# Gathering expert tokens as one native float32 product, a fourth buffer of low halves, and a lookahead that skips unsplit weights

## Chip, cores and metric

One core of one Trainium2 chip. The metric is device microseconds (us) of one execution, the median of the runs. Engines are named as in the profile: PE (TensorE; PEld is its weight load), DVE (VectorE), ACT (ScalarE), POOL, SP (issues DMAs).

## The reference, cut to what matters

Two decoder layers on 256 tokens of width 1024, all float32. Layer 0 is a pooling and sliding-window attention mixer and a dense SwiGLU; layer 1 is a dilated attention and convolution mixer and a mixture of experts. Every sub-layer ends in `x <- LayerNorm(ALPHA * x + f(x))`. The change lies in the mixture of experts:

```
logits = xt @ w_router                          # 8 experts
top_logit, top_e = lax.top_k(logits, 2)
gates = softmax(top_logit)
for each expert e, on the rows xb of the tokens that chose it:
    y = (silu(xb @ w_gate[e]) * (xb @ w_up[e])) @ w_down[e]     # 1024 -> 3584 -> 1024
    out[token] += gate * y
```

All 24 matrices of 8 experts are read from HBM once: 336 pieces of 1 MB.

## The kernel before, in words

**Split products.** A float32 operand is cut into a high half `hi` (rounded to fp32r by a copy on ACT) and a low half `lo = src - hi` (a subtraction on DVE); `split` (lines 126 to 128) does both. A product is then hi·hi + lo·hi + hi·lo, three fp32r matmuls (`mm3`, lines 316 to 319). A *native* product takes float32 operands as they are.

**Weights.** `Weights` streams 128x2048 pieces. `load` issues a DMA on SP into a free `raw` tile; `hi` (L251 to 264; the copy is L259) writes the high half to a ring `wh` of AHEAD + 1 = 4 tiles on ACT; `lo` (the subtraction is L276) writes the low half to a ring `wl` of AHEAD = 3 tiles on DVE, and only then gives the raw tile back to the next DMA. `take` hands a piece to the matmuls, `drop` ends it: it counts `used` up and calls `pump`, which issues one `hi` and one `lo`. This order of issue is the order of work on ACT and on DVE, since the part is scheduled by hand (`tc.manual_schedule`, L1049): each engine runs its instructions in the order of the program. The limits, for a piece k of the experts:

```
            if k in self.native or k not in self.raw or k - self.used > ahead or k >= self.limit:
                return False
...
                if k - self.used < AHEAD - 1 if k >= MOE_BASE else self.step(self.at_lo) != self.at_hi:
                    self.lo()
```

The first is in `hi`, which `pump` calls with `ahead` = 2; the second in `pump`. So `hi` runs up to two pieces beyond `used`, `lo` up to one. Pieces 0 to 3 of the experts are split in two halves each (so `pump` runs twice for them). Twenty of the 336 pieces are *native* (not split; L1225 uses them from the raw tile): the down matrices of every second step of the heavy experts, and one piece of most steps of the last light one.

**Experts.** After routing, experts are sorted by their number of tokens. Expert 0 comes first; those with at most 64 tokens are *light* (five here: 1 to 5), others (0, 6, 7) *heavy*. A step (`Experts.step`) is one 512-wide slice of one expert: two gate pieces, two up pieces, then the two down pieces of the step before. Heavy and light steps alternate in an order fixed by `mixed`. A heavy step ends its up product with a multiplication on DVE (L1438, `h`), and PE transposes `h` after the two down pieces (L1243). In the very first step there is no step before, so the transposes follow at once; behind them DVE runs some 25 small instructions that sort the experts (L1317 to L1355).

**Gather.** A unit (`Unit`, L1162) holds the gathered tokens of one expert, split into high and low halves. A one-hot matrix `oh` of token against slot is the moving operand; the stationary one is a 128x128 block of the tokens. Because the tokens are split once, into `xkh` and `xkl` (two 128x2048 fp32r tiles; L1090, L1092, L1116, L1302), the gather runs twice: a product for the high halves and one for the low halves, each 16 matmuls, all at L1180. A heavy unit does this in four parts with a PSUM bank each (`half`, evacuated by three ACT copies and one DVE copy at L1186), a light one in two (`thin`, two ACT copies at L1191). `Experts.part` runs one part after the gate product and one after the up product of a step. Banks come from a ring of four, shared with the gate and up products, the fold of the light steps (L1237, a native float32 product) and the combine (L1280 to L1282).

**Order around routing.** Lines 1070 to 1118 and 1285 to 1310 lay out by hand the norm of both token halves, the router's transposes and logits, the token splits, and single `W.hi()` and `W.lo()` calls between them. Then `x` is scaled by ALPHA in place (L1323) and collects the experts' results. At the end seven matmuls on `xkh` (L1509) keep PE running before the last merge.

Of the kernel before, what the change touches and what calls it, by code (L numbers as in the profile page):

```python
# [26 lines left out]
PIECE = 2048  # L27
# [61 lines left out]
def trunk(ctx, tc, stream, x_tok, x_t, pos, ln_w, ln_b, pool_bd, pool_sc, sinks, conv_w, router, cf, cb, windows,  # L89
# [64 lines left out]
    class Weights:  # L154
        def __init__(self):
            self.order = []
            self.native, self.base = set(), [0]
            self.raw, self.split, self.loaded = {}, {}, 0
            self.free = [raw1.tile([128, PIECE], F32, name=f"raw{i}") for i in range(RAW1)]
            self.kept = {}  # L160
            self.limit = LIMIT
            self.taken = self.used = 0
            self.at_hi = self.at_lo = (0, 0)

        def follow(self, seq, native=()):
            order = list(range(MOE_BASE + 4))
            for s in range(1, len(seq)):
                order += [(*seq[s], j) for j in range(4)] + [(*seq[s - 1], j) for j in (4, 5)]
            order += [(*seq[-1], j) for j in (4, 5)]
            assert order[:self.loaded] == self.order[:self.loaded]  # L170
            self.order = order
            self.native = {k for k, o in enumerate(order) if o in native}

        def skip(self):
# [76 lines left out]
        def hi(self, ahead=AHEAD):  # L251
            self.skip()
            k, q = self.at_hi
            if k in self.native or k not in self.raw or k - self.used > ahead or k >= self.limit:
                return False
# [27 lines left out]
        def pump(self, n=1, full=False):  # L283
            for _ in range(n):
                self.hi(AHEAD if full else AHEAD - 1)
                k = self.at_lo[0]
                if k - self.used < AHEAD - 1 if k >= MOE_BASE else self.step(self.at_lo) != self.at_hi:
                    self.lo()
# [599 lines left out]
    with tc.tile_pool(name="od1", bufs=1) as e1, tc.tile_pool(name="od2", bufs=2) as e2:  # L888
# [153 lines left out]
    raw3 = ctx.enter_context(tc.tile_pool(name="raw3", bufs=1))  # L1042
    xk, yb = [raw2.tile([128, PIECE], F32R, name=f"xk{i}") for i in range(2)], \
        raw2.tile([128, PIECE], F32R, name="yb")
    raws = [raw3.tile([128, PIECE], F32, name=f"raw{RAW1 + i}") for i in range(RAW2 + RAW3 - 3)]
# [3 lines left out]
    ctx.enter_context(tc.manual_schedule())  # L1049
    xkh, xkl = [t.rearrange("p (i d) -> p i d", i=2) for t in xk]  # L1050
    lgp = bank()
    lg0 = lgp[:, :2 * NE].rearrange("p (i e) -> p i e", e=NE)

    def route(norm, c):
# [10 lines left out]
        return logits  # L1065

    def split_tokens(i):
        split(xkh[:, i], xkl[:, i], x[:, i])

# [19 lines left out]
    lga = route(na, 4)  # L1089
    nc.scalar.copy(xkh[:, 0], x[:, 0])  # L1090
    lgb()
    nc.vector.tensor_sub(xkl[:, 0], x[:, 0], xkh[:, 0].bitcast(F32))  # L1092
    lgb = route(na, 6)
# [21 lines left out]
    keep(KEEP[2])  # L1115
    nc.scalar.copy(xkh[:, 1], x[:, 1])  # L1116
    W.hi()
# [44 lines left out]
    class Unit:  # L1162
# [13 lines left out]

        def gather(self, a, c, b, m):
            for k in range(c, c + 512 // m):
                for i in range(2):
                    nc.tensor.matmul(b[:, (k - c) * m:(k - c + 1) * m],  # L1180
                                     (xkh, xkl)[a][:, i, k * 128:(k + 1) * 128],
                                     self.oh[:, i], start=i == 0, stop=i == 1)

        def half(self, c, a, b, copy):
            self.gather(a, c, b, 128)
            copy(self.xg[a][:, c:c + 4], b.rearrange("p (k s) -> p k s", s=128))  # L1186

        def thin(self, a):
            b = bank()
            self.gather(a, 0, b, LIGHT)  # L1190
            nc.scalar.copy(self.xg[0][:, :, a * LIGHT:(a + 1) * LIGHT], b.rearrange("p (k s) -> p k s", s=LIGHT))  # L1191

        def parts(self):
            yield self.start()
            for j in range(2 if self.light else 4):
                if self.light:
                    self.thin(j)
                else:
                    self.half(4 * (j % 2), j // 2, bank(), nc.vector.tensor_copy if j == 3 else nc.scalar.copy)
                yield  # L1200

# [86 lines left out]
    m2 = ctx.enter_context(tc.tile_pool(name="mo2", bufs=1, side="right"))  # L1288
    rings.add("oh", [m2.tile([128, 2, 128], F32R, name="oh")])
    rings.add("ohb", [m2.tile([128, 2, 128], F32R, name="ohb")])  # L1290
# [7 lines left out]
    rings.add("bank", [bank() for _ in range(4)])  # L1298
    places = [big_tile(t) for t in ("mh", "ml")]
    unit = Unit(places[0], 0, False, slot)  # L1300
    unit.start()
    nc.vector.tensor_sub(xkl[:, 1], x[:, 1], xkh[:, 1].bitcast(F32))  # L1302
    W.lo()
    for c in (0, 4):
        unit.half(c, 0, acc(), nc.scalar.copy)
    for c in (0, 4):
        unit.half(c, 1, bank(), nc.vector.tensor_copy if c == 0 else nc.scalar.copy)
    for _ in range(4):
# [7 lines left out]
    def gates():  # L1316
# [5 lines left out]
        nc.vector.tensor_add(gate, gate, hots[1])  # L1322
        nc.scalar.activation(x, x, AF.Copy, scale=ALPHA)  # L1323

# [178 lines left out]
    def tail(x8):  # L1503
# [4 lines left out]
        for _ in range(7):  # L1508
            nc.tensor.matmul(spare, xkh[:, 0, :128], xkh[:, 0, :512], start=True, stop=True)  # L1509
        e, n, ht = x8.prev  # L1510
# [207 lines left out]
```

## Time and profile before

| | us |
|---|---|
| runs | 1370.35, 1371.65, 1372.81 (median 1371.65) |
| profiled execution, its own time | 1369.15 |
| its span, first to last instruction | 1367.4 |
| mean granted TensorE clock | 0.993 of 2.4 GHz |

The mixer of layer 0, its SwiGLU and the mixer of layer 1 take the first 440 us; routing and the first gather lie at 440 to 470 us; the experts at 470 to 1345 us; the last norm and output after that. In rows of the timeline the columns are start, duration, engine, line, operation, out<-in and shape; what stands in brackets is the idle time of the engine before it and what ended it. In rows by group, the numbers after the bar are total busy time in us and the mean of one in ns, then idle time before.

### The profile page before, as it was taken

To read this page: it belongs to the slowest core of one execution; us is meant where nothing else is said; L and a number is where in the kernel's file an instruction comes from. 1 tells how busy PE (TensorE), PEld (TensorE's weight loads), DVE (VectorE), ACT (ScalarE), POOL (GpSimd) and SP (SyncE) were. 2 spreads that over 40 slices of the span, in tenths; PEclk is the share of its full clock that TensorE was granted. 3 is DMA by queue.
4 is the path that set the end of the run, shared out by engine and by line. 5 is a ranking of instruction groups with operands and counts; after the bars stand their busy time and mean duration, and the time that the engine had idled before them with its cause. 6 is when DMAs were issued, how large, how long until landed. Compare 5 with 4: busy or idle time off the path is not lost.

```text
span 1367.4 us, 19552 instructions
## 1 busy us (share of the span) xinstructions
PE 1334.0 (98%) x7296; PEld 1117.6 (82%) x7296; DVE 1099.9 (80%) x1067; ACT 926.7 (68%) x974; POOL 2.5 (0%) x8
## 2 busy tenths in 40 slices
PE   8999999999999989999999999999999999999995
PEld 6889999988998778887888787887887877877774
DVE  6866555587655788898998898989898989979876
ACT  5745444455643666887886887878787878867673
POOL 0000000000000000000000000000000000000000
PEclk9999999999999999999999999999999999999998
DMA  8616655536425679999999999999999999998990
GB/s 269 238 59 222 214 185 186 185 117 218 144 86 183 259 291 370 371 418 403 420 394 383 365 420 418 419 420 408 390 390 418 418 398 405 419 409 345 402 387 34
DMA packets 72379, 426.69 MB, mean 312 GB/s; under 512 B 8915, under 2 KB 9683, under 8 KB 30549
## 3 DMA queue, kind: packets, MB, share of 16 engines
q1 hardware_dynamic: 71412, 424.35, 79.9%
q0 software_dynamic: 576, 0.62, 0.3%
q8 instruction: 59, 0.97, 0.3%
q10 hardware_dynamic: 288, 0.39, 0.1%
q14 instruction: 44, 0.35, 0.1%
HBM read 424.91 MB, written 1.05 MB: 312 GB/s over the span
## 4 chain that ended last, share of the span: by engine, by line
PE 88%; DVE 6%; ACT 2%; DMA 2%; issue 1%; SPq 0%; ACTq 0%; DVEq 0%
PE bank L319 9%; PE bank L318 9%; PE bank L317 9%; PE bank L1228 8%; PE bank L1227 8%; PE acc L319 5%; PE acc L317 5%; PE acc L318 5%; PE acc L1227 5%; PE acc L1228 4%; PE bank L1237 4%; PE acc L1225 4%; DVE wl L276 3%; DMA raw<-in_stream 2%; PE bank L1180 2%; PE bank L1225 2%
## 5 line engine op out<-in xcount | busy, mean ns | idle before, releaser
L276 DVE TENSOR_TENSOR wl<-raw,wh 128x2048 fp32r<-128x2048 f32 (+2 forms) x453 | 861.8, 1928 | 165.8 <-ACT wh L259 123.6
L259 ACT CAST wh<-raw 128x2048 fp32r<-128x2048 f32 (+2 forms) x455 | 726.9, 1621 | 155.0 <-PE bank L319 62.1
L1227 PE MATMUL bank<-wh,ml 128*128 128x512 f32 x536 | 218.8, 408 | 0.6 <-ACT h L1424 0.6
L1228 PE MATMUL bank<-wl,ml 128*128 128x512 f32 x536 | 210.5, 393 | 2.2 <-DVE wl L276 2.0
L319 PE MATMUL bank<-wl,mh 128*128 128x512 f32 x336 | 132.3, 394 | 3.1 <-DVE wl L276 3.1
L317 PE MATMUL bank<-wh,mh 128*128 128x512 f32 x336 | 133.7, 398 | 0.0
L318 PE MATMUL bank<-wh,mh 128*128 128x512 f32 x336 | 132.0, 393 | 0.0
L1228 PEld LDWEIGHTS bank<-wl,ml 128*128 128x128 f32 x536 | 100.9, 188 | 27.0 <-DVE wl L276 6.6
L1227 PEld LDWEIGHTS bank<-wh,ml 128*128 128x128 f32 x536 | 100.9, 188 | 21.9 <-issue 2.4
L317 PE MATMUL bank<-xth,wh 128*128 128x256 f32 x416 | 118.2, 284 | 0.0
L318 PE MATMUL bank<-xth,wl 128*128 128x256 f32 x416 | 117.7, 283 | 0.0
L319 PE MATMUL bank<-xtl,wh 128*128 128x256 f32 x416 | 117.7, 283 | 0.0
L1227 PE MATMUL acc<-wh,hh 128*128 128x512 f32 (+1 forms) x308 | 114.5, 379 | 0.0
L1228 PE MATMUL acc<-wl,hh 128*128 128x512 f32 (+1 forms) x308 | 112.2, 371 | 0.0
L317 PEld LDWEIGHTS bank<-xth,wh 128*128 128x128 f32 x416 | 79.8, 192 | 0.4
L318 PEld LDWEIGHTS bank<-xth,wl 128*128 128x128 f32 x416 | 79.8, 192 | 0.4
L1237 PEld LDWEIGHTS bank<-cst,h 128*128 128x128 f32 x560 | 73.2, 191 | 8.3 <-ACT wh L259 1.7
L319 PEld LDWEIGHTS bank<-xtl,wh 128*128 128x128 f32 x416 | 79.8, 192 | 0.0
L317 PE MATMUL acc<-wh,hh 128*128 128x512 f32 x200 | 79.4, 398 | 0.0
L318 PE MATMUL acc<-wh,hl 128*128 128x512 f32 x200 | 78.2, 391 | 0.4 <-DVE hl L130 0.4
L319 PE MATMUL acc<-wl,hh 128*128 128x512 f32 x200 | 78.2, 391 | 0.0
L319 PEld LDWEIGHTS bank<-wl,mh 128*128 128x128 f32 x336 | 63.9, 190 | 17.1 <-DVE wl L276 3.5
(280 smaller groups left out, 1877.3 us busy)
## 6 DMA issues: line engine op xcount, KB each, us to landing
raw<-in_stream SPq DMA_DIRECT2D x326, 1024.0 KB, 9.5
raw<-in_stream SPq DMA_DIRECT2D x142, 512.0 KB, 4.7
ln_wb<-in_ln_w SPq DMA_DIRECT2D x3, 512.0 KB, 7.6
ln_wb<-in_ln_b SPq DMA_DIRECT2D x3, 512.0 KB, 8.7
xraw<-in_x_t SPq DMA_DIRECT2D x4, 256.0 KB, 7.4
raw<-in_stream SPq DMA_DIRECT2D x4, 256.0 KB, 5.2
x<-in_x_tok SPq DMA_DIRECT2D x1, 1024.0 KB, 6.5
win<-in_windows SPq DMA_DIRECT2D x1, 768.0 KB, 10.0
```

Of the source, the lines that this page charges most:

```text
L259: nc.scalar.copy(self.split[k][0][:, c], self.raw[k][:, c])
L276: nc.vector.tensor_sub(wl[:, c], self.raw[k][:, c], wh[:, c].bitcast(F32))
L317: nc.tensor.matmul(o, ah, bh, start=start, stop=False)
L318: nc.tensor.matmul(o, al, bh, start=False, stop=False)
L319: nc.tensor.matmul(o, ah, bl, start=False, stop=stop)
L1180: nc.tensor.matmul(b[:, (k - c) * m:(k - c + 1) * m], (xkh, xkl)[a][:, i, k * 128:(k + 1) * 128], self.oh[:, i], start=i == 0, stop=i == 1)
L1225: nc.tensor.matmul(o, a if a.dtype == F32 else a.bitcast(F32), bh, start=start, stop=stop)
L1227: nc.tensor.matmul(o, a, bh, start=start, stop=False)
L1228: nc.tensor.matmul(o, a, bl, start=False, stop=stop)
L1237: nc.tensor.matmul(b[:, k * LIGHT:(k + 1) * LIGHT], h[:, k * 128:(k + 1) * 128], fold, start=True, stop=True)
```

## The change

The tokens are no longer split before the gather. The unsplit `x` (now called `tokens`) is the stationary operand of one native float32 product with a float32 one-hot, and the gathered result is split as it leaves PSUM, with `hi` on ACT and `lo` on DVE. A heavy unit has two parts in place of four, a light one has one in place of two. The first unit's gather uses `bank()` where its high halves used `acc()`. The two tiles `xk` are gone; in their place stand `xsum`, which takes the scaled `x` (so that `tokens` stays as it was), and a fourth tile of the ring `wl`. `pump` lets `lo` go up to two pieces beyond `used`, as `hi` does, in place of one, and both limits count only pieces that are split. The seven matmuls before the last merge read another tile.

```diff
-            self.kept = {}
+            self.kept, self.deep = {}, AHEAD - 1
...
+        def ahead(self, k):
+            return sum(j not in self.native for j in range(self.used, k))
...
-            if k in self.native or k not in self.raw or k - self.used > ahead or k >= self.limit:
+            if k in self.native or k not in self.raw or self.ahead(k) > ahead or k >= self.limit:
...
-                if k - self.used < AHEAD - 1 if k >= MOE_BASE else self.step(self.at_lo) != self.at_hi:
+                if self.ahead(k) < self.deep if k >= MOE_BASE else self.step(self.at_lo) != self.at_hi:
                     self.lo()
...
-    xk, yb = [raw2.tile([128, PIECE], F32R, name=f"xk{i}") for i in range(2)], \
-        raw2.tile([128, PIECE], F32R, name="yb")
+    xsum = raw2.tile([128, 2, D], F32, name="xsum")
+    yb = raw2.tile([128, PIECE], F32R, name="yb")
+    rings.tiles["wl"].append(raw2.tile([128, PIECE], F32R, name=f"wl{AHEAD}"))
+    W.deep = AHEAD
...
-    nc.scalar.copy(xkh[:, 0], x[:, 0])
     lgb()
-    nc.vector.tensor_sub(xkl[:, 0], x[:, 0], xkh[:, 0].bitcast(F32))
...
-    nc.scalar.copy(xkh[:, 1], x[:, 1])
...
-        def gather(self, a, c, b, m):
-            for k in range(c, c + 512 // m):
+        def gather(self, c, b):
+            m = LIGHT if self.light else 128
+            for k in range(512 // m):
                 for i in range(2):
-                    nc.tensor.matmul(b[:, (k - c) * m:(k - c + 1) * m],
-                                     (xkh, xkl)[a][:, i, k * 128:(k + 1) * 128],
+                    nc.tensor.matmul(b[:, k * m:(k + 1) * m], tokens[:, i, (c + k) * 128:(c + k + 1) * 128],
                                      self.oh[:, i], start=i == 0, stop=i == 1)
-
-        def half(self, c, a, b, copy):
-            self.gather(a, c, b, 128)
-            copy(self.xg[a][:, c:c + 4], b.rearrange("p (k s) -> p k s", s=128))
-
-        def thin(self, a):
-            b = bank()
-            self.gather(a, 0, b, LIGHT)
-            nc.scalar.copy(self.xg[0][:, :, a * LIGHT:(a + 1) * LIGHT], b.rearrange("p (k s) -> p k s", s=LIGHT))
+            hi, lo = [t[:, c:c + 512 // m] for t in self.xg] if not self.light else \
+                     [self.xg[0][:, :, a * m:(a + 1) * m] for a in range(2)]
+            split(hi, lo, b.rearrange("p (k s) -> p k s", s=m))
...
         def parts(self):
             yield self.start()
-            for j in range(2 if self.light else 4):
-                if self.light:
-                    self.thin(j)
-                else:
-                    self.half(4 * (j % 2), j // 2, bank(), nc.vector.tensor_copy if j == 3 else nc.scalar.copy)
-                yield
+            for c in (0,) if self.light else (0, 4):
+                yield self.gather(c, bank())
...
-    rings.add("oh", [m2.tile([128, 2, 128], F32R, name="oh")])
+    rings.add("oh", [m2.tile([128, 2, 128], F32, name="oh")])
...
+    tokens, x = x, xsum
     unit = Unit(places[0], 0, False, slot)
     unit.start()
-    nc.vector.tensor_sub(xkl[:, 1], x[:, 1], xkh[:, 1].bitcast(F32))
     W.lo()
     for c in (0, 4):
-        unit.half(c, 0, acc(), nc.scalar.copy)
-    for c in (0, 4):
-        unit.half(c, 1, bank(), nc.vector.tensor_copy if c == 0 else nc.scalar.copy)
+        unit.gather(c, bank())
...
-        nc.scalar.activation(x, x, AF.Copy, scale=ALPHA)
+        nc.scalar.activation(x, tokens, AF.Copy, scale=ALPHA)
...
-            nc.tensor.matmul(spare, xkh[:, 0, :128], xkh[:, 0, :512], start=True, stop=True)
+            nc.tensor.matmul(spare, places[1][:, :128], places[1][:, :512], start=True, stop=True)
```

## Rows read from the trace of the kernel before

**Rows 1.** The page: busy us, share and instructions of each engine.
```profile
PE 1334.0 (98%) x7296; PEld 1117.6 (82%) x7296; DVE 1099.9 (80%) x1067; ACT 926.7 (68%) x974; POOL 2.5 (0%) x8
```

**Rows 2.** Busy us by stage: PE, PEld, DVE, ACT, POOL, then clock, DMA share, GB/s.
```profile
480.00:500.00 20.00, 16.12 (x65) 12.81 (x65) 17.43 (x37) 12.21 (x8) 0.00 (x0) 0.91 0.68 240
...
1000.00:1100.00 100.00, 100.00 (x488) 81.88 (x487) 94.30 (x61) 80.37 (x65) 0.00 (x0) 1.00 1.01 415
```

**Rows 3.** Waits of PE and PEld, 500 to 1345 us: total, times, longest (us).
```profile
PE bank L1228 <- DVE wl L276: 2.0, 4, 0.6
...
PE bank L1227 <- ACT h L1424: 0.6, 1, 0.6
...
PEld bank L1228 <- DVE wl L276: 6.6, 12, 1.1
```

**Rows 4.** Groups of PE by shape, 465 to 1345 us.
```profile
L1237 PE MATMUL bank<-cst,h 128*128 128x64 f32 x560 | 69.9, 268 | 0.0
L1225 PE MATMUL acc<-raw,hf 128*128 128x512 f32 x112 | 50.7, 596 | 0.0
...
L1180 PE MATMUL bank<-oh,xk 128*128 128x64 f32 x160 | 18.7, 272 | 0.0
L1180 PE MATMUL bank<-oh,xk 128*128 128x128 f32 x80 | 10.2, 274 | 1.1 <-DVE sg L1462 0.7 <-ACT h L1436 0.4
```

**Rows 5.** Groups of DVE by shape, 465 to 1345 us.
```profile
L276 DVE TENSOR_TENSOR wl<-raw,wh 128x2048 fp32r<-128x2048 f32 x303 | 682.3, 2284 | 61.5 <-ACT wh L259 37.4 <-issue 15.4 <-PE bank L319 3.8
...
L130 DVE TENSOR_TENSOR hl<-bank,hh 128x512 fp32r<-128x512 f32 x14 | 9.6, 686 | 7.1 <-ACT hh L129 7.0
```

**Rows 6.** Timeline of the end of the mixer, PE and DVE.
```profile
450.81 1.23 DVE L1092 TENSOR_TENSOR xk<-x,xk 128x1024 fp32r<-128x1024 f32 x1 [2.65 <-ACT xk L1090]
...
451.96 1.22 DVE L276 TENSOR_TENSOR wl<-raw,wh 128x1024 fp32r<-128x1024 f32 x1
...
452.40 0.40 PE L319 MATMUL acc<-xth,mh 128*128 128x512 f32 x1
...
453.09 0.68 DVE L423 SCALAR_TENSOR_TENSOR x<-x,acc 128x512 f32<-128x512 f32 x1
```

**Rows 7.** Timeline of the experts' first two steps, ACT, DVE and PE.
```profile
475.86 3.72 ACT L259 CAST wh<-raw 128x2048 fp32r<-128x2048 f32 x2
...
480.23 0.69 DVE L1438 TENSOR_TENSOR h<-h,bank 128x512 f32<-128x512 f32 x1
...
480.97 0.66 PE L1243 MATMUL bank<-cst,h 128*128 128x128 f32 x4 [0.78 <-DVE h L1438]
481.38 0.47 PE L317 MATMUL bank<-wh,mh 128*128 128x512 f32 x1
...
488.33 4.48 DVE L276 TENSOR_TENSOR wl<-raw,wh 128x2048 fp32r<-128x2048 f32 x2
...
490.66 0.79 PE L319 MATMUL bank<-wl,mh 128*128 128x512 f32 x1 [3.10 <-DVE wl L276]
...
495.06 0.40 PE L319 MATMUL bank<-wl,mh 128*128 128x512 f32 x1
```

**Rows 8.** Busy us in three stretches; the number after POOL is the granted clock.
```profile
490.59:493.99 3.40, 3.33 (x8) 2.65 (x9) 3.40 (x3) 0.30 (x1) 0.00 (x0) 0.50 0.72 200
975.28:978.68 3.40, 3.40 (x10) 2.62 (x9) 3.22 (x3) 1.54 (x1) 0.00 (x0) 0.50 1.02 422
978.70:982.10 3.40, 3.40 (x16) 2.79 (x16) 1.86 (x2) 1.91 (x1) 0.00 (x0) 1.00 1.02 424
```

**Rows 9.** Timeline of a later heavy step, ACT, DVE and PE.
```profile
650.91 3.85 ACT L259 CAST wh<-raw 128x2048 fp32r<-128x2048 f32 x2
...
655.80 0.69 DVE L1438 TENSOR_TENSOR h<-h,bank 128x512 f32<-128x512 f32 x1 [0.37 <-PE bank L319]
...
659.23 0.60 PE L1243 MATMUL bank<-cst,h 128*128 128x128 f32 x4
```

**Rows 10.** Timeline of PE in the attention of layer 1.
```profile
423.91 2.57 PE L1014 MATMUL bank<-v,pt 128*128 128x64 f32 x22
```

More of the change, by code (lines that the diff above doesn't have):

```diff
@@ L1049, in trunk @@
     ctx.enter_context(tc.manual_schedule())
-    xkh, xkl = [t.rearrange("p (i d) -> p i d", i=2) for t in xk]
     lgp = bank()
@@ L1065, in route @@
         return logits
-    def split_tokens(i):
-        split(xkh[:, i], xkl[:, i], x[:, i])
     na.add(1, oa[1])
```

## The prediction

> **What bounds the kernel now.** I read the page's engine line first, then busy time by stage, then who waits for whom among the experts, then the timeline around each long wait. The page gives PE 98%, DVE 80%, ACT 68% [rows 1]. By stage the experts differ from the rest: from 1000 to 1100 us PE is busy all the time, DVE 94%, and the DMA engines are full [rows 2]. The reader should see three resources near their limit at once, with PE the one that is never let go: of the 845 us from 500 to 1345, PE's own rows show waits of 2.0 us for a low half of weights and 0.7 + 0.6 + 0.4 us around the gather [rows 3, 4]. A matmul's record overlaps its neighbours (16 of them start in 3.40 us, 0.21 us apart, though each lasts 0.39 or more), so a short wait is hidden in it; the weight loads show 6.6 us in 12 waits for the same low halves [rows 3, 8]. That is the true size from above, and 2.0 from below. Data are not what is missing: no idle time of the low-half group is ended by a DMA [rows 5].
>
> One place outside is worse. In the stage from 480 to 500 us PE is busy only 16.1 of 20 us [rows 2]: it stands 3.10 us for a low half that DVE starts at 488.33, behind the small instructions that sort the experts, and then the granted clock is 0.50, the 1.2 GHz level, for 3.4 us: 8 matmuls start in that stretch where 16 start in a stretch of the same length at 1.00 [rows 7, 8]. So a fall of the clock costs about 8 x 0.21 = 1.7 us there, and (16 - 10) x 0.21 = 1.3 us at 975 us [rows 8].
>
> **The change, part by part.** *The gather on PE: nothing.* A native product is two records on PE: the fold's 280 products (35 light steps, 8 each) stand as 560 [rows 4]. A unit had 16 matmuls for high and 16 for low halves; now it has 16 products of two records, 32 as before. Per record: native with 64 columns 69.9 / 560 = 0.125 us, the gather's own 18.7 / 160 = 0.117 with 64 and 10.2 / 80 = 0.128 with 128 columns [rows 4]. For five light units and three heavy ones the difference is between +1.3 us (5 x 32 x 0.008) and -0.3 us. No row has a native product with 128 columns; it lies between 0.125 (64) and 50.7 / 112 = 0.45 us (512 columns) [rows 4]. A quarter of the latter is 0.11 and so below the 0.125 that the short ones need anyway; I take 0.
>
> The Trainium skill ("FP8 and Floating Point Precision", TensorE Precision Notes) counts four passes through the array for true FP32, which speaks against a native product in place of two fp32r ones. By it the gather would be twice as long; the sum would be that of the third rival below.
>
> *Token splits removed:* two ACT copies and two DVE subtractions. Of these only one is near the path: the subtraction at 450.81 (1.23 us) pushes a low half, which ends at 453.18, and the norm's addition starts at 453.09, though PE was done at 452.40 + 0.40 = 452.80 [rows 6]. Without it the addition starts when PE is done: -0.2 us. The other subtraction and both copies lie beside PE work.
>
> *Evacuation:* a light unit's two ACT copies become one copy and a DVE subtraction, a heavy unit's three copies and a DVE copy become two and two. The subtraction is taken from its like out of PSUM, 0.686 us [rows 5]. DVE gets 7 x 0.686 = 4.8 us more among the later units (five light, two heavy); what hides it is DVE's idle time, 61.5 us before the low halves alone [rows 5]. If that cover is gone, all 4.8 us lie on the path.
>
> *Fewer parts, fewer banks:* a heavy unit takes two banks and two calls in place of four. Three waits go with it: 0.7 us and 0.4 us for a bank of the gather, 0.6 us of the up product for the bank that the gate copy on ACT had not left [rows 3, 4]. All three lie at the two heavy units, so with the third and fourth parts gone I take all 1.7 us. The longest of them stands just before the clock falls at 975.28 [rows 8]; without it PE has no break there, and I take that fall's 1.3 us too. Together -3.0; the bounds are 0 and -3.0.
>
> *The low halves one piece earlier.* By the pump's rule, in the first step `used` goes to 3 and then 4; before, the low halves of pieces 4 and 5 were issued there, now those of 4, 5 and 6. Piece 6 is the one that PE stood 3.10 us for. But its subtraction now stands ahead of the multiplication `h` on DVE's queue. Its high half is done at 475.86 + 3.72 = 479.58, DVE is free at 480.2, so it ends near 482.4, and `h` moves from 480.23 to 482.35: 2.1 us later. The transposes wait for that, as in this step no down product stands between: PE stands 0.8 + 2.1 = 2.9 us there, and the second step begins at 481.38 + 2.1 = 483.5 [rows 7]. Piece 7's first matmul with a low half is that step's 39th. Before, the 26th ended at 490.66 - 3.10 = 487.56 and so started 0.4 us earlier, at 487.16; 25 steps from 481.38 make 0.23 us each, and 38 of them 8.7 us: PE reaches the 39th at 492.2, while DVE, whose small instructions shift by 2.1 us too, has it at 488.33 + 2.1 + 2.3 = 492.7. Before it was at 495.06 [rows 7]. That is -2.4 us if the clock holds. As a stand of 3.10 us was followed by a fall, I expect one after 2.9 us too: 492.2 + 1.7 = 493.9, which is -1.2. So the wait is not removed, it moves to the transposes; I take -1.2, bounds 0 and -2.4.
>
> In the rest, a low half needs its high half, and that needs a tile of the ring of four that PE has left; so the fourth low tile gives up to one piece, 2.28 us, of lead, but in light stretches less. Where DVE has a run of other work ahead of a low half (halves of `h`, one-hots), the order now puts the low half first. Natives no longer count, so after them three pieces are ready. Against it stand DVE's 4.8 us. Of the waits between 2.0 and 6.6 us I take 2.2, near PE's own rows, as these are the ones that PE surely sees.
>
> *Sum:* -0.2 - 3.0 - 1.2 - 2.2 = -6.6 us. The profiled execution would go from 1369.15 to 1362.5 us. That execution is 2.5 us under the median of the runs, 1371.65, and 1.2 under the lowest; the forecast of the median is 1371.65 - 6.6 = 1365.0 us.
>
> **The rivals.** *DVE gives it back* (no change): DVE is at 94% in its fullest stage [rows 2], the lead is used up by the seven subtractions, and the waits for low halves stay. Then -0.2 - 1.2 - 1.7 = -3.1, less what 4.8 us more of DVE adds to its lateness; with a quarter of it, 1.2 us, that is 1369.7 us. For it speaks the 94%, against it the 61.5 us of idle time [rows 5].
>
> *The multiplication falls behind* (slower): in 20 later heavy steps, too, `h` now stands behind one more low half. At 655.80 it ends at 656.49 and PE transposes it at 659.23, 2.74 us later; the high half before it ends at 654.76 and the subtraction at 657.1, so `h` would end at 657.8, with 1.4 us left [rows 9]. The mechanism decides from there: if DVE is one more low half behind (2.2 us), PE stands 0.8 us in each of 20 steps, 16 us, and the time is 1381 us. For it speaks DVE's load, against it the margin.
>
> *The native product costs its passes* (slower): 64 records a unit in place of 32, 0.11 us each, for eight units: +28 us, 1393 us. Against it stand the fold's 560 records [rows 4].
>
> *The merged light gather cools the clock* (no change): a light unit now runs 32 short matmuls in one row, some 3.6 us, where it had two runs of 1.9. If the clock fell in each of five, at 1.5 us (between the 1.7 and 1.3 above), 7.5 us would be lost: 1372.5 us. Against it: 22 short native matmuls in 2.57 us in the attention were not followed by a fall [rows 10].
>
> **How the numbers follow.** The forecast gets 0.67, DVE giving it back 0.17, the clock 0.06, the multiplication 0.06, the passes 0.04. The likeliest time is 1365.0. Its best case (-0.2 - 3.0 - 2.4 - 6.6) would be 1359.5; the range goes from 1360.0 up to 1371.5, which takes in the first rival and a median that repeats the one before. Two tenths of a per cent, 2.7 us, is about what a measurement here can tell from no change. Faster by more than that: the forecast and a little of the first rival, 0.69; within it: 0.21; slower: 0.10.
>
> **What would show it.** Right: L1180's line has as many records as before at 0.12 to 0.13 us; the wait of 3.10 us is gone, and one of about 2.9 us stands before the first transposes, perhaps with the clock at 0.50 behind it; no wait of PE for a bank around the two heavy gathers, no fall of the clock there; fewer than 12 waits of the weight loads for low halves; transposes of later heavy steps that wait for nothing. Wrong: the same 6.6 us of waits (the first rival), waits of the transposes in every heavy step (the second), twice the records in the gather (the third), or the clock at 0.50 after light gathers (the fourth).

## The result and the profile after

**1403.04 us** (median of 4 runs, 1402.52 to 1403.53) against 1372.23 us for the kernel before in runs beside it (1370.35 to 1375.34): ratio 1.0222 [1.0202, 1.0242]. The forecast was 1365.0 us with a range up to 1371.5, so it was wrong by its sign: 31 us were lost where 6.6 were to be gained. No rival of the prediction gives the mechanism either; the second comes nearest, a multiplication on DVE behind one more low half, but it names another multiplication.

The page of the kernel after, busy time of each engine and then the shares of the chain that ended last:

```profile
PE 1344.1 (96%) x7296; PEld 1119.8 (80%) x7296; DVE 1101.1 (79%) x1073; ACT 915.9 (65%) x964; POOL 2.5 (0%) x8
...
PE 69%; DVE 15%; issue 6%; DMA 5%; ACT 5%; SPq 0%; ACTq 0%; DVEq 0%
```

Against [rows 1], PE has the same 7296 records and is busy 10.1 us longer, and of the span of 1401.6 us it is idle 57.5 where it was idle 33.4 of 1367.4: +24.1. Together that is the loss of 34.2 us in span. DVE is busy 1.2 us longer and ACT 10.8 us less, so it is not work that was added: the work stands apart in time. Part of PE's 10.1 us is the clock, which from 480 us to the last merge falls to 0.50 five times in place of two. The waits of 500 to 1385 us, all engines (total, times, longest), which answer to [rows 3]:

```profile
DVE wl L279 <- ACT wh L262: 104.6, 70, 2.6
ACT hh L1449 <- DVE sg L1448: 96.5, 28, 4.9
...
PEld bank L1225 <- ACT h L1410: 11.5, 6, 2.5
...
PE bank L1225 <- ACT h L1410: 9.0, 6, 2.1
...
PE bank L1231 <- DVE h L1424: 5.9, 10, 0.9
...
PE bank L1269 <- DVE yb L130: 4.4, 3, 2.3
...
PEld bank L1216 <- DVE wl L279: 3.5, 11, 0.5
```

The same two pairs of ACT and DVE in the kernel before, 500 to 1385 us:

```profile
DVE wl L276 <- ACT wh L259: 41.4, 27, 5.4
ACT hh L1463 <- DVE sg L1462: 37.4, 28, 4.0
```

The waits for low halves at the weight loads did fall, from 6.6 to 3.5 us in the row shown (at L1215 four more waits, 3.0 us, are put down to low halves; four of the same length stood there before under "issue"). In their place PE stands for ACT's gate copy `h` in light steps, for DVE's `h` in heavy ones, and for `yb`. Away from PE, two waits grew from 79 to 201 us: DVE for the high half that it is to subtract, and ACT, at the light step's copy `hh`, for DVE's multiplication `sg`. Each engine waits for the other.

One light step shows how. The kernel after, timeline of ACT from 586.4 us (start, duration, what; in brackets the idle time before and what ended it):

```profile
586.47 3.72 ACT L262 CAST wh<-raw 128x2048 fp32r<-128x2048 f32 x2
593.33 0.41 ACT L1449 CAST hh<-sg 128x256 fp32r<-128x256 f32 x1 [3.14 <-PE bank L1216]
593.64 3.70 ACT L262 CAST wh<-raw 128x2048 fp32r<-128x2048 f32 x2
597.25 0.58 ACT L1410 COPY h<-bank 128x512 f32<-128x512 f32 x1
```

The same stretch on DVE:

```profile
588.41 4.50 DVE L279 TENSOR_TENSOR wl<-raw,wh 128x2048 fp32r<-128x2048 f32 x2 [1.11 <-ACT wh L262]
592.83 0.41 DVE L1448 TENSOR_TENSOR sg<-sg,bank 128x256 f32<-128x256 f32 x1
595.58 2.29 DVE L279 TENSOR_TENSOR wl<-raw,wh 128x2048 fp32r<-128x2048 f32 x1 [2.34 <-ACT wh L262]
```

and on PE:

```profile
597.87 1.11 PE L1225 MATMUL bank<-cst,h 128*128 128x64 f32 x8 [1.83 <-ACT h L1410]
```

Read it in order. The last down piece's pump issues a high half on ACT and, on DVE, the low half of that same piece; only then comes `sg` on DVE (592.83), and `hh` on ACT waits for it (593.33, after 3.14 us of nothing). The next high half stands behind `hh` on ACT, and the next low half on DVE waits for that (2.34 us of nothing). So first ACT idles for DVE and then DVE for ACT. The gate copy stands behind two high halves, and PE's fold comes 1.83 us late for it. The bracket puts ACT's idle time down to PE's bank, but `hh` starts just behind the end of `sg` (592.83 + 0.41 = 593.24 us). In the kernel before, only one low half stood between, the one whose high half is the first of the two on ACT. ACT there, and then DVE:

```profile
582.45 3.72 ACT L259 CAST wh<-raw 128x2048 fp32r<-128x2048 f32 x2
587.11 0.41 ACT L1463 CAST hh<-sg 128x256 fp32r<-128x256 f32 x1 [0.94 <-DVE sg L1462]
```

```profile
584.39 2.29 DVE L276 TENSOR_TENSOR wl<-raw,wh 128x2048 fp32r<-128x2048 f32 x1 [0.44 <-ACT wh L259]
586.60 0.41 DVE L1462 TENSOR_TENSOR sg<-sg,bank 128x256 f32<-128x256 f32 x1
```

The first steps went much as forecast (a stand of 3.35 us, 2.9 forecast). PE and the clock there and at the second fall (columns as in [rows 2]):

```profile
485.61 0.66 PE L1231 MATMUL bank<-cst,h 128*128 128x128 f32 x4 [3.35 <-DVE h L1424]
```

```profile
486.21:489.62 3.41, 3.41 (x10) 2.64 (x9) 2.39 (x13) 3.31 (x3) 0.00 (x0) 0.50 1.02 428
598.85:602.26 3.41, 3.41 (x10) 2.68 (x9) 3.41 (x2) 2.84 (x3) 0.00 (x0) 0.50 0.90 312
602.26:605.67 3.41, 3.41 (x20) 2.96 (x19) 3.24 (x3) 3.13 (x3) 0.00 (x0) 1.00 1.03 370
```

And the gather, which answers to [rows 4]:

```profile
L1179 PE MATMUL bank<-oh,x 128*128 128x64 f32 x160 | 18.4, 273 | 0.0
L1179 PE MATMUL bank<-oh,x 128*128 128x128 f32 x96 | 11.8, 278 | 1.7 <-DVE oh L1168 1.7
```

As many records as before (16 of the 96 stood under the tile `acc` there, beside the 80 of [rows 4]), at 18.4 / 160 = 0.115 and 11.8 / 96 = 0.123 us each. The later heavy gathers now wait for their one-hots, 0.52 us twice.

### The profile page after: what moved, and what is told of

Same layout as the page of the kernel before. It is cut to its first block, busy times and chain, and to the rows that moved or that the text cites. A ratio compares the mean times of both kernels' runs of the same rounds, so it can differ in the third digit from the quotient of the medians.

```text
span 1401.6 us, 19428 instructions
## 1 busy us (share of the span) xinstructions
PE 1344.1 (96%) x7296; PEld 1119.8 (80%) x7296; DVE 1101.1 (79%) x1073; ACT 915.9 (65%) x964; POOL 2.5 (0%) x8
## 4 chain that ended last, share of the span: by engine, by line
PE 69%; DVE 15%; issue 6%; DMA 5%; ACT 5%; SPq 0%; ACTq 0%; DVEq 0%
DVE wl L279 10%; PE bank L321 7%; PE bank L320 7%; PE bank L322 7%; PE bank L1215 6%; PE bank L1216 6%; DMA raw<-in_stream 5%; PE acc L322 5%; PE acc L320 5%; PE acc L321 5%; PE acc L1213 3%; PE bank L1225 3%; ACT wh L262 3%; PE acc L1215 3%; PE acc L1216 2%
## 5 line engine op out<-in xcount | busy, mean ns | idle before, releaser
L1215 PE MATMUL bank<-wh,ml 128*128 128x512 f32 x536 | 221.9, 414 | 0.0
L1216 PE MATMUL bank<-wl,ml 128*128 128x512 f32 x536 | 214.6, 400 | 0.4 <-DVE wl L279 0.4
L1215 PEld LDWEIGHTS bank<-wh,ml 128*128 128x128 f32 x536 | 102.7, 192 | 21.7 <-issue 2.4
L1215 PE MATMUL acc<-wh,hh 128*128 128x512 f32 (+1 forms) x308 | 114.6, 379 | 0.0
L1449 ACT CAST hh<-sg 128x256 fp32r<-128x256 f32 x35 | 14.2, 406 | 120.0 <-DVE sg L1448 96.5
L1225 PE MATMUL bank<-cst,h 128*128 128x64 f32 x560 | 70.7, 269 | 10.3 <-ACT h L1410 9.0
L321 PE MATMUL acc<-wh,hl 128*128 128x512 f32 x200 | 78.2, 391 | 0.4 <-DVE hl L130 0.4
```

The lines of the kernel that those rows point to most:

```text
L321: nc.tensor.matmul(o, al, bh, start=False, stop=False)
L1215: nc.tensor.matmul(o, a, bh, start=start, stop=False)
L1216: nc.tensor.matmul(o, a, bl, start=False, stop=stop)
L1225: nc.tensor.matmul(b[:, k * LIGHT:(k + 1) * LIGHT], h[:, k * 128:(k + 1) * 128], fold, start=True, stop=True)
L1449: nc.scalar.copy(ht[:, :, :LIGHT], s3)
```

## The experiments

Two theories at first. **A**: the deeper lookahead of low halves closes a circle of the two waits seen above. **B**: the gather itself (native products, its splits on ACT and DVE) makes the loss. Medians are given with the ratio to the kernel before in runs beside it.

### The parts, one at a time

**Gather alone** (both limits of the pump as before):

```diff
-            if ... self.ahead(k) > ahead or k >= self.limit:
+            if ... k - self.used > ahead or k >= self.limit:
...
-                if self.ahead(k) < self.deep if k >= MOE_BASE else ...
+                if k - self.used < AHEAD - 1 if k >= MOE_BASE else ...
```

> The changed kernel with both limits of the pump as they were before: the native gather, the split behind it and the fourth low tile stay, but a low half is again issued one piece behind its high half and natives are counted. Theory A (a circle of waits between ACT and DVE: at the end of a light step the product sg stands on DVE behind a low half, that low half waits for the high half issued just before it on ACT, and ACT's copy hh waits for sg with the next high half behind it): 1366 to 1371 us, the idle time of ACT before hh that is ended by sg falls from 96.5 us back to about 37 us, and the waits of the fold for ACT (9.0 us) are gone. Theory B (the gather itself: native products, later evacuation, 4.8 us more on DVE): 1395 to 1405 us.

Measured: 1370.95 us, 0.9990 [0.9975, 1.0004]. B falls. PE's waits from 500 to 1345 us are all in two rows, none for a bank at a heavy gather (against [rows 3]), and the clock does not fall near 975 us:

```profile
PE bank L1216 <- DVE wl L279: 2.9, 6, 0.6
PE bank L1225 <- ACT h L1410: 0.5, 1, 0.5
```

**Counting only split pieces** (the line `W.deep = AHEAD` left out, so low halves run one piece beyond `used`):

> The changed kernel with the limit of the low halves as before (one piece beyond used); natives are not counted. Theory A: the low half is behind its high half by one piece outside the natives, so 1366 to 1373 us. Theory B: 1395 to 1405 us. If not counting natives is what costs (high halves of later pieces ahead of copies that PE waits for): 1380 to 1400 us.

Measured: 1371.32 us, 0.9991 [0.9978, 1.0005]. The new way of counting is not the cause. Yet ACT stands long for `sg` here too, 500 to 1345 us:

```profile
ACT hh L1448 <- DVE sg L1447: 70.5, 33, 4.0
```

So a long wait of ACT is not yet a loss.

**Depth alone** (`k - self.used` in both limits, but the low halves' limit `self.deep`, 3 in place of 2):

> The changed kernel with natives counted as before; only the low halves go one piece further. Theory A: nearly the whole loss, 1395 to 1405 us, with ACT idle before hh for 80 us or more. Theory B: 1395 to 1405 us too; if the natives carry the loss: 1366 to 1375 us.

Measured: 1401.42 us, 1.0203 [1.0177, 1.0230]. The loss is here: one number, the depth of low halves.

### The order

**`sg` ahead of the pump** (the full change otherwise):

```diff
                 finish(down_half(self.y[pe], pht, 1, pn, W.take(None)))
+                if light:
+                    nc.vector.tensor_mul(sg, sg, b[:, 4 * LIGHT:])
                 W.drop()
...
             if light:
-                nc.vector.tensor_mul(sg, sg, b[:, 4 * LIGHT:])
```

> The whole change, but in light steps the product sg is issued before the drop of the last down piece, so that it stands ahead of the low half on DVE. Theory A: the circle is cut in the light steps; ACT's idle time before hh ended by sg falls below 40 us and the time to 1368 to 1380 us (the 3.4 us before the first transposes and those before the later ones stay). Theory B: no change, 1398 to 1405 us.

Measured: 1369.08 us, 0.9970 [0.9954, 0.9986]: 34 us less than the change by moving one instruction of 0.41 us ahead of one of 2.29, and faster than the kernel before. DVE in the same light step, which now has one low half fewer ahead of `sg` (two stand behind it):

```profile
587.90 0.41 DVE L1441 TENSOR_TENSOR sg<-sg,bank 128x256 f32<-128x256 f32 x1
588.23 4.73 DVE L279 TENSOR_TENSOR wl<-raw,wh 128x2048 fp32r<-128x2048 f32 x2
```

ACT in that step (its wait for `sg` is 0.94 us, not 3.14):

```profile
588.41 0.41 ACT L1450 CAST hh<-sg 128x256 fp32r<-128x256 f32 x1 [0.94 <-DVE sg L1441]
```

The waits of the transposes in the later heavy steps (5.9 us) go with it, though nothing was changed there: they follow from what happens in the light steps.

**Where: depth in heavy steps only, in light steps only.** Low halves run two pieces beyond `used` in one kind of step (one more is issued at its start), one piece in the other (the run for light steps has `True` in the place of `False`):

```diff
             light = unit.light
+            if light == False:
+                W.deep = AHEAD
+                W.lo()
+            else:
+                W.deep = AHEAD - 1
```

> Edit: the full change, but low halves run two pieces beyond used only within heavy steps (one more is issued when a heavy step begins); in light steps they run one piece beyond, as in the kernel before. Theory (the loss is made in light steps, by the circle between sg on DVE and hh on ACT): the circle cannot close, so 1368 to 1374 us, and ACT's waits of hh for sg near 45 us. Rival (the loss is made in heavy steps, where the multiplication h stands behind one more low half): 1390 us or more, with the waits of the transposes for h still there.

> Edit: the reverse; two pieces beyond used within light steps, one within heavy steps. Theory: nearly the whole loss stays, 1392 to 1404 us, ACT's waits of hh for sg near 85 to 97 us. Rival: 1368 to 1376 us.

Measured: heavy only 1368.73 us, 0.9972 [0.9959, 0.9985]; light only 1407.27 us, 1.0258 [1.0233, 1.0282], 3 us above the range given for it. The loss belongs to the light steps. In the heavy steps, where the prediction had looked for it, the depth costs nothing that shows.

**One place only.** The gather alone with one line before `sg` in light steps:

```diff
+                W.lo()
                 nc.vector.tensor_mul(sg, sg, b[:, 4 * LIGHT:])
```

> Edit: the gather's change with the limits of the kernel before (1370.95 us in its run), and one line more: at the end of a light step one low half is issued just ahead of sg, so that the lookahead is one piece deeper at that one place, 35 times, and falls back with the next piece. Theory (the place of sg behind a low half whose high half was just issued is what costs): 20 us or more of the loss come with that one line, 1390 to 1405 us. Rival (the depth costs in more places, by what it does to ACT and the transposes in all steps): under 10 us, up to 1380 us.

Measured: 1403.77 us, 1.0238 [1.0206, 1.0270]. One low half, 35 times, and the whole loss is there. ACT's waits for `sg`, 500 to 1345 us:

```profile
ACT hh L1450 <- DVE sg L1449: 96.6, 28, 6.2
```

One light step of this run on DVE, ACT and PE:

```profile
589.12 6.68 DVE L279 TENSOR_TENSOR wl<-raw,wh 128x2048 fp32r<-128x2048 f32 x3
595.72 0.41 DVE L1449 TENSOR_TENSOR sg<-sg,bank 128x256 f32<-128x256 f32 x1
596.22 0.40 ACT L1450 CAST hh<-sg 128x256 fp32r<-128x256 f32 x1 [4.13 <-DVE sg L1449]
600.76 1.39 PE L1225 MATMUL bank<-cst,h 128*128 128x64 f32 x8 [2.83 <-ACT h L1410]
```

Here none of the three low halves ahead of `sg` waits for its high half: they run back to back. That the low half's high half was just issued, as the theory has it, is not what makes `sg` late in this step: the 6.68 us of low halves ahead of it do.

### Why the low half is late, and how the loss reaches PE

**A fifth tile of high halves in place of the fourth of low halves**, high halves one piece further ahead, `sg` behind the pump:

```diff
-    rings.tiles["wl"].append(raw2.tile([128, PIECE], F32R, name=f"wl{AHEAD}"))
-    W.deep = AHEAD
+    rings.tiles["wh"].append(raw2.tile([128, PIECE], F32R, name="wh4"))
...
-            if ... self.ahead(k) > ahead or k >= self.limit:
+            if ... self.ahead(k) > ahead + self.more or k >= self.limit:
...
         if s == 0:
+            W.deep, W.more = AHEAD, 1
+            W.hi()
+            W.lo()
```

> Edit: the full change with sg in its place behind the pump, but the additional tile is a fifth of high halves in place of a fourth of low halves, and high halves run one piece further (three beyond used). So as many low halves stand ahead of sg as in the change, but the high half that each one needs was issued a piece earlier. Theory (a circle: sg waits for a low half that waits for the high half issued beside it): without the adjacency the loss goes, 1366 to 1373 us. Rival (load alone: sg is late because one more low half of 2.28 us stands ahead of it): the loss stays, 1390 us or more.

Measured: 1398.90 us, 1.0177 [1.0149, 1.0206]. The theory's number failed. The waits, 500 to 1385 us, show why this run could not tell:

```profile
ACT hh L1448 <- DVE sg L1447: 88.0, 24, 4.9
DVE wl L279 <- PE bank L1215: 18.5, 9, 4.9
DVE wl L279 <- PE bank L322: 17.2, 26, 5.8
DVE wl L279 <- ACT wh L262: 15.0, 13, 2.4
```

DVE waits little for ACT's high half now (15.0 us, 104.6 in the change); it waits for PE to leave a low tile (18.5 + 17.2 us), of which there are three. So the adjacency of low and high half went, but another wait came in its place, and the run does not tell load from adjacency.

**Both tiles** (a fourth of low halves as well, one raw tile fewer to make room):

> Edit: as five_high, and the fourth tile of low halves stays too; the room for it is one raw tile fewer. In five_high the low half ahead of sg waited for a tile that PE had to leave, in place of waiting for a high half (17.7 + 17.2 us of DVE's waits of that kind), so it could not tell. Here neither should be waited for. Theory (sg is late because the low half ahead of it cannot start yet): 1366 to 1376 us, ACT's waits of hh for sg near 40 us. Rival (2.28 us more of DVE work ahead of sg are enough): 1390 us or more, waits near 80 us. If waits for the missing raw tile (DMA) show, between the two.

Measured: 1370.45 us, 0.9983 [0.9965, 1.0001]. The loss is gone with `sg` in its late place. But the waits did not fall as far as expected (500 to 1345 us):

```profile
ACT hh L1449 <- DVE sg L1448: 72.0, 33, 4.0
DVE wl L279 <- ACT wh L262: 13.8, 8, 2.9
DVE wl L279 <- PE bank L322: 3.8, 9, 0.4
```

ACT still stands 72.0 us for `sg`, far above the 42.7 of the gather alone, and PE hardly notices (1.1 us of waits for the gate copy). DVE's wait back for ACT is down to 13.8 us. Whether that, or the high half's additional lead, is what spares the kernel is not shown: the run that only counts otherwise stood 70.5 us without any additional lead and lost nothing.

**ACT's copy `hh` one piece later** (the full change, `sg` in its late place):

```diff
-                nc.scalar.copy(ht[:, :, :LIGHT], s3)
-                self.late = lambda: nc.vector.tensor_sub(ht[:, :, LIGHT:], s3, ht[:, :, :LIGHT].bitcast(F32))
+                self.late = lambda: split(ht[:, :, :LIGHT], ht[:, :, LIGHT:], s3)
```

> Edit: the full change with sg in its place, but ACT's copy hh, which waits for sg, is issued one piece later, behind the next high half, together with its subtraction. Theory (the loss reaches PE through ACT, which stands for sg with the next high half and the gate copy h behind it): ACT no longer stands there, 1366 to 1376 us. Rival (DVE itself is what is late, ACT's stand is only its sign): 1390 us or more, with waits of low halves and of the transposes.

Measured: 1372.09 us, 1.0009 [0.9992, 1.0026]. The chain is cut on ACT's side, with `sg` still behind the same low halves, and the loss is gone; ACT's waits for `sg` are 37.3 us, as in the kernel before (37.4). `hh` is not needed before the next step's down pieces, so the copy had no reason to stand ahead of the next high half.

**What separates the runs with the loss from those without.** ACT's idle time ahead of `hh`, whatever the profile says ended it, DVE's waits for high halves, and the fold's waits for the gate copy (us, 500 to 1385, the last two columns to 1345 in runs without the loss):

| kernel | ACT ahead of `hh` | DVE for high halves | PE for gate copy |
|---|---|---|---|
| after | 120.0 | 104.6 | 9.0 |
| fifth high tile | 125.8 | 15.0 | 12.0 |
| depth in light steps only | 123.9 | 80.9 | 10.2 |
| one place only | 118.6 | 67.7 | 11.2 |
| depth alone | 113.1 | 108.8 | 9.0 |
| both tiles | 78.2 | 13.8 | 1.1 |
| only split pieces counted | 72.5 | 34.3 | 0.5 |
| depth in heavy steps only | 67.0 | 40.0 | 0.5 |
| `sg` ahead | 60.5 | 60.4 | 0 |
| gather alone | 54.2 | 47.4 | 0.5 |
| before | 50.9 | 41.4 | 0 |
| `hh` later | 42.5 | 62.8 | 0 |

The first five lose, the others do not. The first and the last column part the two groups, the middle one does not. So the path that the runs show goes one way: one more low half ahead of `sg`, ACT late at `hh`, the gate copy behind it late, PE late at the fold. That DVE's wait back for ACT, the other half of the circle, is needed for the loss is not shown.

### What is left to gain

**`yb` ahead of the pump too.** With `sg` moved, PE's largest wait from 500 to 1345 us is the combine's:

```profile
PE bank L1269 <- DVE yb L130: 4.8, 5, 1.4
```

In this run `split_y(...)` of a finished expert also stands ahead of `W.drop()`:

> Edit: the light step's multiplication sg stands ahead of the pump, and so do the two splits of a finished expert's result (yb). Theory (what DVE and ACT have in hand for PE must stand ahead of the next pair of high and low halves): the combine's five waits for yb (4.8 us in the run with sg alone moved) go to under 1.5 us, and the time falls from 1369.1 by 3 to 5 us, to 1364 to 1366 us. Rival (the waits only move, since a split ahead of the pump makes the next halves later): the 4.8 us reappear as waits for low halves or for h, and the time stays within 1.5 us of 1369.1.

Measured: 1368.76 us, 0.9980 [0.9966, 0.9994]. The waits for `yb` are gone; 1.9 us of waits for the copy `oht` and 1.9 for the combine's sum on DVE stand in their place. The rival's time was right; the waits moved, though to other places than it named.

**The first steps.** Depth one piece in step 0, and piece 6's low half issued between the transposes and the sort (`W.lo()` and then `W.deep = AHEAD` ahead of `gates()`); the same together with `yb`; and that with `W.hi()` and `W.lo()` for piece 7 as well:

> Edit: sg ahead of the pump; and in the first step the lookahead of low halves is one piece, as in the kernel before, while piece 6's low half is issued right behind that step, between the transposes' split and the sort of the experts. Theory (the wait of 3.4 us before the first transposes and the fall of the clock behind it are a matter of order alone): both go, the wait of 3.1 us of the kernel before does not come back, and the time falls from 1369.1 by 3 to 5 us, to 1364 to 1366 us. Rival (the lateness is handed on): PE waits 2 to 3 us for piece 7's low half instead, with a fall of the clock behind it, and the time is 1367.5 to 1370.

> Edit: both of the above. If the two gains are independent they add up: 6 to 10 us below 1369.1, 1359 to 1363 us, which is faster than both the kernel before and every run so far. If something else bounds the experts (the stream of weights from memory, which moves 415 GB/s in the fullest stage) the time stops at 1364 or above and PE's waits stand elsewhere.

> Edit: sg and yb ahead of the pump, and behind the first step the low half of piece 6 and both halves of piece 7 before the experts are sorted. Theory (the stand of 2.6 us for piece 7's low half and the fall of the clock behind it, 1.7 us, are still a matter of order): both go, 3 to 5 us less than the run without piece 7's halves (1367.4), so 1362.5 to 1364.5 us. Rival (handed on again): PE waits for piece 8's low half, behind the sort, for 1 us or more, and the time is 1365.5 to 1368.

Measured: 1368.61 us, 0.9988 [0.9973, 1.0003]; 1367.44 us, 0.9982 [0.9963, 1.0001]; 1369.51 us, 0.9983 [0.9970, 0.9996]. None came near the times of its theory: the first two lie where their other branch put them, the third 1.5 us above its rival's range. The stand is handed on: 3.37 us before the transposes became 2.61 us for piece 7's low half, and in the last of them this, 2.10 us for piece 8's:

```profile
497.99 0.71 PE L322 MATMUL acc<-wl,hh 128*128 128x512 f32 x1 [2.10 <-DVE wl L279]
```

The sort, 5.4 us of small DVE instructions, stood ahead of some piece's low half in every order tried.

**The order without the depth** (`sg` ahead of the pump, limits of the kernel before):

> Edit: the order of sg_first with the limits of the kernel before (low halves up to one piece beyond used, unsplit pieces counted); gather and fourth tile stay. It tells whether the deeper lookahead of low halves is worth anything once the order is right. If depth brings its own gain: 2 us or more above sg_first's 1369.1, so 1371 to 1373 us. If only the order counts: within 1.5 us of 1369.1, and the fourth tile is idle weight. If depth still costs: below 1367.

Measured: 1371.50 us, 0.9994 [0.9978, 1.0011], against 0.9970 [0.9954, 0.9986] with the depth. The two intervals overlap, so the medians don't settle it. Profiled executions differ in the time that they take ahead of the experts (479.5 to 482.9 us in the table), for reasons that nothing here explains. The profiled executions' stretch of the experts alone (from the end of the last matmul ahead of the first transposes to the wait of the last merge that every kernel has) leaves that out:

| kernel | experts' stretch, us | against before |
|---|---|---|
| before | 1349.73 - 480.19 = 869.5 | |
| after | 1383.94 - 482.26 = 901.7 | +32.1 |
| gather alone | 1350.08 - 481.44 = 868.6 | -0.9 |
| only split pieces counted | 1352.73 - 482.66 = 870.1 | +0.5 |
| `hh` later | 1350.04 - 479.51 = 870.5 | +1.0 |
| both tiles | 1349.60 - 482.88 = 866.7 | -2.8 |
| `sg` ahead, no depth | 1347.59 - 480.17 = 867.4 | -2.1 |
| `sg` ahead (full change) | 1347.59 - 480.50 = 867.1 | -2.4 |
| depth in heavy steps only | 1348.26 - 481.76 = 866.5 | -3.0 |
| `sg`, piece 6 | 1347.98 - 480.18 = 867.8 | -1.7 |
| `sg`, `yb` | 1346.54 - 479.74 = 866.8 | -2.7 |
| `sg`, `yb`, piece 6 | 1348.14 - 482.26 = 865.9 | -3.7 |
| `sg`, `yb`, pieces 6 and 7 | 1349.79 - 482.73 = 867.1 | -2.5 |

By these single executions the depth is worth 0.3 us once the order is right, and the order 1.2 without the depth; depth in heavy steps alone, with the order as it was, is worth 2.1 against the gather alone. The kernels with `sg` ahead lie between -1.7 and -3.7, with a fall of the clock or without, so differences of 1 us or so are not settled here. Four kernels are faster than the one before by more than their intervals leave open: `sg` ahead, depth in heavy steps only, `sg` with `yb`, and that with pieces 6 and 7; the first two by 0.3%. Which of them is the fastest stays open.

## Why the prediction was wrong

**The step that failed** is "The low halves one piece earlier", in its part on the rest: "Where DVE has a run of other work ahead of a low half (halves of `h`, one-hots), the order now puts the low half first", and 2.2 us gained. The order was read as a gain for the low half, and its price was followed for one instruction only, `h` in the 20 later heavy steps (the second rival). The same pump stands ahead of `sg` in 35 light steps. There the price is not 2.28 us against a margin on DVE, because ACT waits for `sg` with the next high halves and the gate copy behind it in a queue that runs in order, and PE's fold waits for that copy: 120.0 us of ACT's idle time ahead of `hh` (50.9 before) and 9.0 us of waits of the fold (none before). The runs put +33.1 us of the experts' stretch (901.7 against 868.6 with the gather alone) in the place of -2.2: depth alone 1.0203, one low half ahead of `sg` 1.0238, and each mend of it (`sg` ahead, `hh` later, a tile more on both sides) back to 0.997 to 1.001.

**A sign that was there.** The waits of ACT for `sg` stood in the trace before, 37.4 us in 28 waits; they were not among the rows of the prediction. Such waits of an engine beside the path cost nothing as long as what stands behind them has slack (70.5 us in the run that counts only split pieces), and then they do (96.5 us in the change). The depth was taken for slack, but in this order it gave ACT none: the low half moved up to its own high half and ahead of the multiplication that ACT waits for.

**The signs that the prediction set** came out right for most of their own parts, and none of them watched the light steps. One failed: transposes of later heavy steps do wait, 5.9 us in 10 steps. Two are thin: 11 waits of the weight loads for low halves in the row that had 12, and banks, for which PE still stands 0.7 us twice near the heavy gathers of the change (not with the gather alone).

- *The gather on PE: nothing.* Right; native records with 128 columns cost 0.123 us, inside the 0.11 to 0.125 of the bounds, and a product leaves two of them, as in the fold [rows 4]. The Trainium skill ("FP8 and Floating Point Precision", TensorE Precision Notes) counts four passes through the array for true FP32. At 64 and 128 columns these don't show as time here: two records of 0.115 and 0.123 us, against two fp32r matmuls of 0.117 and 0.128 [rows 4]. At 512 columns they may: a record takes 0.45 us [rows 4], where fp32r matmuls start 0.23 us apart, so two records last as long as four of these.
- *Token splits removed, -0.2.* Right at its place: the norm's addition starts 0.04 us after the end of PE's last matmul (456.63 for 456.19 + 0.40), 0.29 us in the kernel before. In the time ahead of the experts this is lost in the 3 us by which executions differ.
- *Evacuation, 4.8 us hidden.* Right in size: the subtraction takes 0.688 us (0.686 was taken). With the gather alone the time does not rise.
- *Fewer banks, -3.0.* Right in place, over-sized in effect: the three bank waits and the clock's fall at 975 us are gone, but the experts' stretch shrinks by 0.9 only with the gather alone. Of the rest, waits for low halves are 2.9 in place of 2.0, the fold waits 0.5 once, and the first transposes 1.15 in place of 0.78: 1.8 us come back.
- *Step 0, -1.2.* Near: the stand before the transposes was 3.35 us (2.9 was taken) with a fall behind it, for 0.78 + 3.10 before.
- *The multiplication falls behind* (second rival). Its waits are there, but 5.9 us in 10 steps where 16 us in 20 were priced, and as a consequence of the light steps: with depth in heavy steps alone they are absent.
- *DVE gives it back, the passes, the clock after light gathers*: none of them. The clock fell at 598.8, 725.1, 827.5 and 1209.8 us, each time behind a stand of PE for `h` or `yb`.

What the measured sizes leave of the forecast without the failed step: -0.2 - 0.9 for what is not depth, and for depth, step 0 included, -0.3 (with `sg` ahead) to -2.1 us (in heavy steps only), by single executions. That is -1.4 to -3.2 us, at most half of the 6.6.

## What to carry to other kernels

When a change moves an instruction ahead on one in-order queue, list everything behind it there, and for each item who waits for it and what is queued behind that waiter; do it for every kind of step, not only for the one on the path. When a consumer's buffer is made deeper, look whether its producer is deeper too: here low halves without deeper high halves waited 104.6 us for them, and with both a piece deeper 13.8. What another engine is waiting for goes ahead of the prefetch: here one such move of a 0.41 us instruction was worth 34 us.

## What the runs showed that was not expected

The length of a wait beside the path does not tell its cost: the 122 us that ACT and DVE waited longer for each other went with 24 us of idle PE, while 70.5 and 72.0 us of ACT's waits for `sg` (37.4 before) went with no loss in two other kernels. And a stand of PE alone does not tell whether the clock falls: in the kernel after, stands of 1.83, 2.03, 2.06, 2.29 and 3.35 us were each followed by a stretch at 0.50, and one of 2.34 us at 1286.8 us was not:

```profile
1286.79:1290.20 3.41, 3.41 (x9) 1.78 (x10) 1.29 (x1) 2.09 (x2) 0.00 (x0) 1.00 0.84 334
```

In two runs whose first steps are the same, a stand of some 2.6 us for piece 7's low half was followed by a fall in the one and not in the other, which has the shortest stretch of the table. Busy time in a stretch behind that stand, first with `sg` and piece 6, then with `yb` too (columns as in [rows 2]):

```profile
494.49:497.90 3.41, 3.41 (x9) 2.63 (x8) 3.41 (x3) 2.19 (x2) 0.00 (x0) 0.50 0.87 358
```

```profile
495.30:498.70 3.40, 3.38 (x15) 2.81 (x16) 3.40 (x2) 3.07 (x3) 0.00 (x0) 1.00 0.63 222
```

Nine matmuls start in the one and fifteen in the other.
